# Retention decay and norm scale moved from q and k to v's rows and the group norm's epsilon, with three edits to the feed-forward jobs

## The chip, the cores and the metric

One Trainium2 chip, one core, one launch. Of the core's engines five appear in the profile: TensorE (matmuls PE, weight loads PEld), VectorE (DVE), ScalarE (ACT), GpSimd (POOL) and SyncE (SP, which only issues transfers). The metric is the device time of a launch in microseconds; lower is better. Everything is fp32; for speed, most matmul operands are split into a high and a low fp32r part, and a product is three matmuls (high x high, high x low, low x high).

## What is computed

Two decoder layers over 544 tokens: a prompt of 512 and 8 sample sequences of 4 tokens. Layer 0 mixes by a short gated convolution, layer 1 by retention; each is followed by a gated feed-forward block. The part that the change touches is the retention layer's mixer:

```python
def retention_chunkwise(q, k, v, s0):
    log_g = jnp.log(1.0 - 2.0 ** (-5.0 - jnp.arange(H)))
    decay = jnp.where(diff >= 0, jnp.exp(jnp.maximum(diff, 0.0) * log_g), 0.0)
    ...
    scores = jnp.einsum('bhid,bhjd->bhij', qc, kc) * decay
    inner = jnp.einsum('bhij,bhjv->bhiv', scores, vc)
    cross = jnp.einsum('bhid,bhdv->bhiv', qc, S) * cross_w
    S_new = S * chunk_decay + jnp.einsum('bhjd,bhjv->bhdv', kc * state_w, vc)

def retention_mixer(x, s0, pos, w_in, gn_g, w_out):
    q, k, v, g = jnp.split(x @ w_in, ...)          # 4 heads; dk 256, dv 512
    q = rotary(q, pos)
    k = rotary(k, pos) * (HEAD_DK ** -0.5)
    o, S = retention_chunkwise(q, k, v, s0)
    mu, var = mean(o), mean((o - mu) ** 2)          # over a token's dv of a head
    of = (o - mu) * rsqrt(var + GN_EPS)             # GN_EPS = 1e-6
    return (silu(g) * (of * gn_g)) @ w_out, S
```

The input `x` is already normalized: every row of a token was multiplied by that token's rms factor. The decay between tokens i and j is a power of the head's gamma with exponent i - j, so it can be written as a factor of token i times a factor of token j.

## The kernel before

Activations are kept transposed (feature rows on the 128 partitions, 544 tokens along the free dimension, in two halves of 272). The rms factor is not applied to the input: products are made of the raw residual (times gain), and the factor R (128x2x272, one value per token, the same in each row) or rN (one column per tile of 128 tokens) is multiplied in behind the product.

**Who orders the work.** The program names what each engine does; a planner of the framework simulates it, sets the order of each engine's instructions and places the waits. Each engine then runs its own list strictly in order, and an instruction that waits holds up all behind it on that engine. A tile's tag names a ring of buffers; a new tile waits until the buffer's former readers are done. `tc.issue_after` only orders instructions of one engine.

**PSUM.** Eight banks: `psum()` takes a tile of two banks from a ring of two ("mm" in the profile), `bank()` one from a ring of four ("sm").

**The feed-forward jobs.** Gate and up products run as `Job`s: two 128-wide slices of the output at once by a scheme of seven half products in place of eight (numbers 1 to 7, 12 matmuls each, L480). `weights7` (L428) loads the two weight pieces w3 (L434) and w1 (L435), forms three differences and sums on VectorE (L438 to L440: the halves of w2, and one in place) and w4 (L441, which reads w1), and splits all four into high and low parts: `mixed` (ACT L423, DVE L424, ACT L425 and an adding DMA of POOL, L426) for w1 and w3, `split` (ACT L190, DVE L191) for w2 and w4. A job holds three sums: a (products 1, 6, 7, 4), b (product 2) and c (products 5, 3). `summed` (L533) snapshots the first three states of a (u1 to u3, ACT L540) and adds b or c to a snapshot (DVE L543). The sum c22 reads c before product 3 is added into it. In `run` (L516), a job's `prepare` (its weights) is called before the middle of the job ahead, and its first product before the end of that job.

**The stage `ahead`** (L785), at the end of layer 0's feed-forward block, makes what the retention layer will need: q and k of head 0 (four weight pieces, raw products copied to DRAM as `qk_made`), and, as five jobs, gates of heads 0, 1 and 2 (`gates`, L833; L847 multiplies with R).

**The retention heads** (loop at L1298). For head h:
- `qk_start` loads a table gt = gtab[h] (L915; 2 x 544 values in each of 128 rows, 544 KB: decay of q and of k by token), `qk_scale` multiplies its two halves by R (L942). `qk_project` projects a 128-wide piece of q or k, `qk_rotate` multiplies it out of PSUM by gt (L959), and after the second piece `rotate` makes four products with cos and sin (L969 to L972), a difference and a sum (L973, L974). For head 0, `qk_loaded` loads the raw q and k (L926), multiplies by gt (L930) and rotates, k in two halves of the tokens.
- `value` (L987) projects v into four banks, and multiplies by rN as it is split (L1037, L1038). Inside it come the scores of the sample tokens (L1198), qm (L1019) and `keys`.
- `states_update` (L1238 on TensorE, L1243 on VectorE) updates the sample states through two `psum()` tiles; `scores`, `inner` and `normalized` (group norm; the reciprocal root is an add on VectorE, L226, and a power on GpSimd, L227) make the prompt's outputs; `gated` transposes them (L1172) and multiplies by the gate.
- k and q of head h+1 are projected in between (`fill`, and after the third `inner`).

## Time and profile before

| what | value |
|---|---|
| time, median of 3 runs | 1458.92 us (1457.52 to 1459.11) |
| profiled execution: time | 1461.27 us |
| profiled execution: span of its instructions | 1459.5 us |
| mean granted TensorE clock | 0.996 |
| DMA | 201.89 MB, mean 138 GB/s |

The time of a run is a little longer than the span from the first to the last instruction. A row of a timeline has start, duration, engine, line, operation, names (out<-in), shapes, and in brackets the idle time of the engine before it with what ended that. A row by line or tile has minimum, median and maximum duration in ns after the count. A row of waits has the total, the number and the longest. A row of DMA issues has the count, the size of one and the median time from issue to landing. A matmul's recorded duration overlaps the next one's; the distance of starts tells its pace.

### The profile page before, as it was taken

What the parts mean: (1) busy time and instruction counts of PE and PEld (TensorE: products, weight loads), DVE (VectorE), ACT (ScalarE), POOL (GpSimd) and SP (SyncE); (2) the same over time, 40 slices, a digit from 0 to 9 for tenths busy, and PEclk for the clock granted to TensorE, in tenths of its full rate; (3) what the DMA queues carried; (4) which work ended last, traced back from release to release, by engine and by line L of the source; (5) the groups of instructions that cost most, each with busy time, mean ns of one, the idle gap of its engine ahead of it and who ended that gap; (6) DMA issues with size and microseconds to landing.
All of it is one profiled execution on the core that took longest, in us unless ns stands there. A gap on an engine that the chain in (4) does not pass through costs nothing.

```text
span 1459.5 us, 26302 instructions
## 1 busy us (share of the span) xinstructions
PE 1443.8 (99%) x10860; PEld 1369.0 (94%) x10860; DVE 985.7 (68%) x1536; ACT 664.0 (45%) x971; POOL 147.9 (10%) x184
## 2 busy tenths in 40 slices
PE   9999999999999999999999999999999999999997
PEld 8999999999999999997878888878999999999997
DVE  5644679847748648677575765845699848749554
ACT  5222466626526437664223032134386626537334
POOL 0100011101101003210010000000111101101002
PEclk9999999999999999999999999999999999999998
DMA  6222246636536434767353734724666635546432
GB/s 219 82 88 92 86 114 140 150 116 126 143 106 139 124 80 133 195 167 262 125 191 116 258 106 144 274 92 143 175 138 149 153 108 131 131 109 148 119 81 77
DMA packets 84297, 201.89 MB, mean 138 GB/s; under 512 B 8129, under 2 KB 25409, under 8 KB 83921
## 3 DMA queue, kind: packets, MB, share of 16 engines
q1 hardware_dynamic: 67296, 165.91, 35.9%
q0 software_dynamic: 15008, 29.18, 12.2%
q10 hardware_dynamic: 1872, 5.12, 0.9%
q8 instruction: 85, 1.39, 0.4%
q14 instruction: 36, 0.29, 0.1%
HBM read 175.11 MB, written 25.08 MB: 137 GB/s over the span
## 4 chain that ended last, share of the span: by engine, by line
PE 89%; DVE 5%; DMA 3%; ACT 1%; issue 1%; POOL 0%; SPq 0%; DVEq 0%; ACTq 0%; POOLq 0%
PE sm L480 35%; PE mm L175 33%; PE sm L175 7%; PE sm L999 2%; PE sm L1000 2%; PE sm L1001 2%; PE sm L163 2%; PE sm L164 1%; PE sm L165 1%; PE sm L1222 1%; DMA w<-in_ffgu_dram 1%; DVE wl L191 1%; DMA w<-in_rtg_dram 1%; DVE S L1243 1%; DVE ol L191 1%
## 5 line engine op out<-in xcount | busy, mean ns | idle before, releaser
L190 ACT ACTIVATE wh<-w 128x1024 fp32r<-128x1024 f32 (+4 forms) x126 | 115.8, 923 | 318.8 <-PE mm L175 204.9
L480 PE MATMUL sm<-oh,wh 128*128 128x272 f32 x744 | 215.5, 290 | 0.1
L480 PE MATMUL sm<-ol,wh 128*128 128x272 f32 x744 | 214.3, 288 | 0.7 <-DVE ol L191 0.7
L480 PE MATMUL sm<-oh,wl 128*128 128x272 f32 x744 | 213.9, 287 | 0.0
L175 PE MATMUL mm<-xh,wh 128*128 128x272 f32 x844 | 176.3, 290 | 1.1 <-ACT wh L190 1.0
L175 PE MATMUL mm<-xh,wl 128*128 128x272 f32 x844 | 174.5, 289 | 0.4 <-DMA wl<-in_rtqk_dram 0.4
L175 PE MATMUL mm<-xl,wh 128*128 128x272 f32 x844 | 173.9, 287 | 0.0
L480 PE MATMUL sm<-oh,h 128*128 128x272 f32 x568 | 164.1, 289 | 0.5 <-DVE gate L543 0.4
L480 PE MATMUL sm<-oh,l 128*128 128x272 f32 x568 | 163.5, 288 | 0.0
L480 PE MATMUL sm<-ol,h 128*128 128x272 f32 x568 | 163.5, 288 | 0.0
L273 DVE TENSOR_TENSOR x<-x,mm 128x544 f32<-128x544 f32 x90 | 64.7, 719 | 144.7 <-PE mm L175 144.7
L191 DVE TENSOR_TENSOR wl<-w,wh 128x1024 fp32r<-128x1024 f32 (+4 forms) x126 | 134.2, 1071 | 23.7 <-ACT wh L190 22.3
L480 PEld LDWEIGHTS sm<-oh,wh 128*128 128x128 f32 x744 | 139.8, 188 | 2.1 <-ACT gate L540 0.9
L423 ACT ACTIVATE wh<-w 128x1024 fp32r<-128x1024 f32 x97 | 102.8, 1060 | 83.2 <-PE sm L480 56.1
L480 PEld LDWEIGHTS sm<-ol,wh 128*128 128x128 f32 x744 | 139.8, 188 | 0.9 <-DVE ol L191 0.9
L480 PEld LDWEIGHTS sm<-oh,wl 128*128 128x128 f32 x744 | 140.3, 189 | 0.0
L426 POOL DMA_DIRECT2D wl<-in_ffgu_dram x87 | 75.6, 869 | 635.2 <-ACT wl L425 261.5
L175 PEld LDWEIGHTS mm<-xh,wh 128*128 128x128 f32 x844 | 132.2, 188 | 5.4 <-ACT wh L190 1.4
L175 PEld LDWEIGHTS mm<-xh,wl 128*128 128x128 f32 x844 | 131.6, 188 | 0.9 <-DMA wl<-in_rtqk_dram 0.6
L175 PEld LDWEIGHTS mm<-xl,wh 128*128 128x128 f32 x844 | 132.1, 188 | 0.1
L191 DVE TENSOR_TENSOR l<-w,h 128x1024 fp32r<-128x1024 f32 x98 | 93.4, 955 | 27.0 <-ACT h L190 26.4
L480 PEld LDWEIGHTS sm<-oh,h 128*128 128x128 f32 x568 | 107.2, 189 | 1.0 <-ACT wh L423 0.6
(296 smaller groups left out, 3211.8 us busy)
## 6 DMA issues: line engine op xcount, KB each, us to landing
w<-in_ffgu_dram SPq DMA_DIRECT2D x88, 512.0 KB, 3.9
wl<-in_ffgu_dram POOLq DMA_DIRECT2D x87, 256.0 KB, 4.8
w<-in_ffdn_dram SPq DMA_DIRECT2D x96, 192.0 KB, 2.5
S<-in_rets_dram SPq DMA_DIRECT2D x16, 1024.0 KB, 7.0
out_rets_dram<-S SPq DMA_DIRECT2D x16, 1024.0 KB, 4.8
w<-in_cvin_dram SPq DMA_DIRECT2D x21, 512.0 KB, 3.4
w<-in_rtqk_dram SPq DMA_DIRECT2D x16, 512.0 KB, 3.6
w<-in_rtg_dram SPq DMA_DIRECT2D x16, 512.0 KB, 4.1
```

Source lines behind the costliest of these rows:

```text
L163: nc.tensor.matmul(out, lh, rh, start=start, stop=False, skip_group_check=True)
L164: nc.tensor.matmul(out, lh, rl, start=False, stop=False, skip_group_check=True)
L175: last_product[0] = nc.tensor.matmul(half(pt, hf)[:, :HT], w[:, c], act[k][:, hf * HT : (hf + 1) * HT], start=(first and k == ks[0] and i ...
L190: h = nc.scalar.activation(dh, src, AF.Copy)
L191: last_low[0] = nc.vector.tensor_sub(dl, src, dh.bitcast(F32))
L273: last_residual[0] = nc.vector.tensor_add(xk, xk, p)
L423: nc.scalar.activation(wh, w, AF.Copy)
L426: nc.gpsimd.dma_start(wl[:, n:], src[:, n:], accum_op=ALU.add)
L480: last = nc.tensor.matmul(out, w[:, c], b, start=(first and k == 0 and i == 0), stop=(k == KP - 1 and i == 2), skip_group_check=True,)
L999: nc.tensor.matmul(out, xh[kt][:, ts_], wh[:, cw], start=(kt == 0), stop=False)
L1000: nc.tensor.matmul(out, xh[kt][:, ts_], wl[:, cw], start=False, stop=False)
L1001: last = nc.tensor.matmul(out, xl[kt][:, ts_], wh[:, cw], start=False, stop=(kt == KT - 1))
```

## The change

The rms factor and the decay are no longer multiplied into q and k. Rotated q and k stay raw. A row (token) of v is multiplied by its own rms factor, by k's decay and 1/16, and by the rms factor that k's row lacked (`fv`, one column for each of the four token tiles and the sample). A token's output then lacks its q factor; since the group norm divides it out again, only its epsilon is scaled, by the reciprocal of that factor squared (`fe`). For the sample tokens, whose states come from outside, q's factor `gs` is kept and multiplied into qm and the sample scores.

```diff
-    nc.vector.memset(expo, -0.5)
+    nc.vector.memset(expo[:, :6], -0.5)
+    nc.vector.memset(expo[:, 6:], -1.0)
...
-    def rsqrt(out, var, n):
-        nc.vector.tensor_scalar_add(out, var, EPS)
+    def rsqrt(out, var, n, eps=None):
+        if eps is None:
+            nc.vector.tensor_scalar_add(out, var, EPS)
+        else:
+            nc.vector.tensor_add(out, var, eps)
...
     def weights7(src1, src2, sw, adding=False):
-        w3, w1 = [wts.tile([P, 2 * n], F32, tag="w", name=nm("w")) for _ in range(2)]
+        w1, w3 = [wts.tile([P, 2 * n], F32, tag="w", name=nm("w")) for _ in range(2)]
...
-        w4 = sw.tile([P, n], F32, tag="w4", name=nm("w4"))
-        last_load[0] = nc.sync.dma_start(w3, src2)
-        last_load[0] = nc.sync.dma_start(w1, src1)
+        w4 = fourth[0].tile([P, n], F32, tag="w4", name=nm("w4"))
+        second_load[0] = nc.sync.dma_start(w1, src1)
+        last_load[0] = nc.sync.dma_start(w3, src2)
...
                 elif which == 5:
-                    self.c = bank()[:, :HT]
+                    self.c = self.third()[:, :HT]
...
+            fourth[0] = c1.enter_context(tc.tile_pool(name=f"ffw{layer}", bufs=2, reuse_waits="tile"))
...
+        ft = tp.tile([P, 3, P], F32, tag="gu", name=nm("ft"))
+        for t in range(4):
+            nc.sync.dma_start(ft[t * NH : (t + 1) * NH, 0, :], a["gtab"][:, 0, 1, t * P : (t + 1) * P])
+        for t in range(4):
+            nc.sync.dma_start(ft[:NH, 1, t * NS : (t + 1) * NS], a["gtab"][:, 0, 1, SEQ:])
+
+        def factors():
+            pt = bank()
+            nc.tensor.transpose(pt[:, : 4 * NH], ft[: 4 * NH, 0, :], ident[: 4 * NH, : 4 * NH])
+            nc.tensor.transpose(pt[:, 4 * NH : 5 * NH], ft[:NH, 1, :], ident[:NH, :NH])
+            tab = pt[:, : 4 * NH].rearrange("p (t h) -> p t h", h=NH)
+            ri = ft[:, 2, :4]
+            nc.gpsimd.tensor_tensor(ri, rN[:, :4], expo[:, 6:7].to_broadcast([P, 4]), op=ALU.pow)
+            scale, back = [r.unsqueeze(2).to_broadcast([P, 4, NH]) for r in (rN[:, :4], ri)]
+            nc.vector.tensor_mul(fv[:, :4, :], tab, scale)
+            nc.vector.tensor_scalar(
+                fv[:, 4, :], pt[:, 4 * NH : 5 * NH], rN[:, 5:6], rN[:, 5:6], op0=ALU.mult, op1=ALU.mult
+            )
+            nc.vector.tensor_mul(fe, tab, back)
+            nc.vector.scalar_tensor_tensor(fe, fe, 256.0 * EPS, fe, op0=ALU.mult, op1=ALU.mult)
+            nc.vector.tensor_mul(fv[:, :4, :], fv[:, :4, :], scale)
...
-            return Job([a["rtg"][h, n + i] for i in range(2)], operand, sw, summed(tile2, gate))
+            return Job([a["rtg"][h, n + i] for i in range(2)], operand, sw, summed(tile2, gate), lambda: psum()[:, 0, :])
...
-        run(jobs, (2, 5, 6), lambda i: None, iter(()))
+        run(jobs, (2, 5, 6), lambda i: factors() if i == 1 else None, iter(()))
...
-        def qk_start(h):
+        def qk_places(h):
...
-            with tc.issue_after(last_load[0].ins) if h == 0 else ExitStack():
-                nc.sync.dma_start(gt, a["gtab"][h])
...
         def qk_loaded(st):
             for t, src in ((st["rot"][1], qk_made[1]), (st["rot"][0], qk_made[0])):
-                with tc.issue_after(last_load[0].ins):
+                with tc.issue_after((second_load if src is qk_made[1] else last_load)[0].ins):
                     nc.sync.dma_start(t, src)
             for which in (1, 0):
-                qk_scale(st, which)
                 r = st["rot"][which]
-                nc.vector.tensor_mul(r, r, st["gt"][:, which, :].unsqueeze(1).to_broadcast([P, 2, T]))
...
-        def qk_scale(st, which):
-            gi = halves(st["gt"][:, which, :])
-            nc.vector.tensor_mul(gi, gi, R)
...
-            each(
-                lambda p, ri, gi: nc.vector.tensor_mul(ri, p, gi), pt, halves(r[:, dt, :]), halves(st["gt"][:, which, :])
-            )
+            if dt == 0:
+                st["rt"] = products()
+            for d, by in ((st["rt"][1 - dt], sin), (r[:, dt, :], cos)):
+                each(lambda p, d, f: nc.vector.tensor_mul(d, p, f), pt, halves(d), halves(by))
             if dt:
-                rotate(r, *products())
+                turned(r, *st["rt"])
...
+        def turned(r, t0, t1):
             nc.vector.tensor_sub(r[:, 0, :], r[:, 0, :], t0)
             nc.vector.tensor_add(r[:, 1, :], r[:, 1, :], t1)
...
+                    gs = st["gs"] = one.tile([P, NS], F32, tag="gs", name=nm("gs"), bufs=1)
+                    nc.vector.tensor_mul(
+                        by_sequence(gs), by_sequence(R[:, 1, HT - NS :]), fq[:, h, :].unsqueeze(1).to_broadcast([P, NB, DS])
+                    )
...
-                nc.scalar.activation(vh[:, tt, :], pv[tt], AF.Copy, scale=rN[:, tt : tt + 1])
+                nc.scalar.activation(vh[:, tt, :], pv[tt], AF.Copy, scale=fv[:, tt, h : h + 1])
...
+            nc.vector.tensor_mul(ss, ss, st["gs"][:NS])
...
+        fq = one.tile([P, NH, DS], F32, tag="fq", name="fq")
+        nc.sync.dma_start(fq, a["gtab"][:, :, 0, SEQ : SEQ + DS].rearrange("h p s -> p h s"))
...
-            yn0 = normalized(inner(h, st, 0))
+            yn0 = normalized(inner(h, st, 0), fe[:, 0, h : h + 1])
```

The sample's v (`v4`), the low half of v, the other three prompt norms and qm follow the same pattern; two small tiles that shared a buffer (tag "vs") move with it to another pool, which keeps the pools' sizes in line with those of the stage before. Four loads of gt, every L942 and both L930 are gone, the job's third sum takes a tile of the wide ring in the gate jobs of `ahead` alone, and the order of the two weight loads and the second place for w4 hold for all jobs, those of both feed-forward blocks too.

More of the change, by code (lines that the diff above doesn't have):

```diff
@@ L127, in hybrid_decode_kernel @@
     rN = resid.tile([P, 6], F32, tag="rN", name="rN")
-    last_load = [None]
+    fv = resid.tile([P, 5, NH], F32, tag="fv", name="fv")
+    fe = resid.tile([P, 4, NH], F32, tag="fe", name="fe")
+    last_load, second_load = [None], [None]
     def parts2(n, pool=None, tags=("wh", "wl")):
@@ L461, in hybrid_decode_kernel, with __init__ @@
     class Job:
-        def __init__(self, srcs, operand, sw, take):
-            self.srcs, self.operand, self.sw, self.take = srcs, operand, sw, take
+        def __init__(self, srcs, operand, sw, take, third=None):
+            self.srcs, self.operand, self.sw, self.take, self.third = srcs, operand, sw, take, third or bank
         order = (6, 5, 2)
@@ L1058, in keys @@
                 nc.tensor.transpose(pt[:NS, 0, token_tiles(dt)], krot[:, dt, SEQ:], ident)
-            k2 = qp.tile([NS, 2, 2 * P], F32R, tag="vs", name=nm("k2"), bufs=1)
+            k2 = one.tile([NS, 2, 2 * P], F32R, tag="vs", name=nm("k2"), bufs=1)
             split(k2[:, 0, :], k2[:, 1, :], pt[:NS, 0, : 2 * P])
@@ L1091, in sample_operands @@
             placed(pt[:, 1, : 2 * P], k2[:, 0, :], k2[:, 1, :], 1)
-            vs = qp.tile([P, DV], F32R, tag="vs", name=nm("vs"), bufs=1)
+            vs = one.tile([P, DV], F32R, tag="vs", name=nm("vs"), bufs=1)
             nc.scalar.activation(vs, pt[:, 0, :], AF.Copy)
@@ L1326, in hybrid_decode_kernel @@
                 nc.sync.dma_start(st["gate"][0][:, :2, :], gate_made[0][:, :2, :])
-                nxt = qk_start(1)
-                for which in (1, 0):
-                    qk_scale(nxt, which)
+                nxt = qk_places(1)
             fill(2)
@@ L1339, in hybrid_decode_kernel @@
                 held_parts(h, older)
-            yn0 = normalized(inner(h, st, 0))
+            yn0 = normalized(inner(h, st, 0), fe[:, 0, h : h + 1])
             sample_outputs(h, st, 1)
-            yn1 = normalized(inner(h, st, 1))
+            yn1 = normalized(inner(h, st, 1), fe[:, 1, h : h + 1])
             states_update(h, st, 1)
@@ L1346, in hybrid_decode_kernel @@
             if more and h:
-                nxt = qk_start(h + 1)
-                for which in (1, 0):
-                    qk_scale(nxt, which)
+                nxt = qk_places(h + 1)
             with tc.issue_after(last_product[0].ins):
```

35 lines of the change are left out of this document (17 added, 18 removed).

## The prediction

> **What bounds the kernel now.** I read the page first: the engines' shares and the chain that ended last.
>
> ```profile
> span 1459.5 us, 26302 instructions
> PE 1443.8 (99%) x10860; PEld 1369.0 (94%) x10860; DVE 985.7 (68%) x1536; ACT 664.0 (45%) x971; POOL 147.9 (10%) x184
> PE 89%; DVE 5%; DMA 3%; ACT 1%; issue 1%; POOL 0%; SPq 0%; DVEq 0%; ACTq 0%; POOLq 0%
> ```
>
> TensorE carries 89% of the chain and idles 1459.5 - 1443.8 = 15.7 us. An edit that takes work from VectorE or a DMA queue is worth only what TensorE waited for it, so I looked for TensorE's idle time in the stages that the change touches: the work for the next layer at the end of the first feed-forward block (about 560 to 656 us), then the four retention heads. The view by stretches has busy time of PE, PEld, DVE, ACT, POOL, then clock, DMA share and GB/s.
>
> ```profile
> 560.00:656.00 96.00, 93.46 (x718) 91.51 (x718) 73.57 (x123) 66.70 (x101) 20.38 (x20) 0.98 0.66 179
> 656.00:1050.00 394.00, 393.74 (x2543) 324.69 (x2541) 255.41 (x395) 114.44 (x151) 17.50 (x22) 1.00 0.51 171
> ```
>
> The heads leave 394.00 - 393.74 = 0.26 us idle: where most of the edited lines run there is almost nothing to win, only something to lose. The stage ahead leaves 2.54 us, at a clock of 0.98. TensorE's timeline has three waits there:
>
> ```profile
> 592.28 0.52 PE L175 MATMUL mm<-xh,wl 128*128 128x272 f32 x2 [0.36 <-DMA wl<-in_rtqk_dram]
> ...
> 626.75 0.29 PE L480 MATMUL sm<-xh,wl 128*128 128x272 f32 x1
> 627.41 0.36 PE L480 MATMUL sm<-oh,h 128*128 128x272 f32 x1 [0.37 <-DVE gate L543]
> ...
> 632.67 0.29 PE L480 MATMUL sm<-ol,wh 128*128 128x272 f32 x1
> 632.80 0.29 PE L480 MATMUL sm<-oh,wl 128*128 128x272 f32 x1
> 634.88 0.39 PE L480 MATMUL sm<-xh,h 128*128 128x272 f32 x1 [1.80 <-DVE gate L543]
> ```
>
> Starts normally stand 0.13 us apart, so the third wait costs 634.88 - 632.80 - 0.13 = 1.95 us and the second 627.41 - 626.75 - 0.13 = 0.53 us. The third has a tail: from about 636.0 the clock reads 0.50 for 3.4 us and starts stand 0.225 us apart.
>
> ```profile
> 636.00:639.40 3.40, 3.40 (x18) 3.40 (x17) 3.15 (x6) 1.35 (x2) 0.02 (x1) 0.50 0.69 105
> ...
> 637.08 0.43 PE L480 MATMUL sm<-oh,l 128*128 128x272 f32 x1
> 637.30 0.43 PE L480 MATMUL sm<-oh,h 128*128 128x272 f32 x1
> ```
>
> In 3.4 us go 3.4 / 0.225 = 15 matmuls, each 0.10 us late: 1.5 us more. So 1.95 + 1.5 + 0.53 = 4.0 us hang on two waits.
>
> Why the third happened stands in VectorE's timeline just before, and in SP's:
>
> ```profile
> 625.09 0.69 DVE L441 TENSOR_TENSOR w<-w,w 128x512 f32<-128x512 f32 x1
> 625.70 1.22 DVE L191 TENSOR_TENSOR l<-w,h 128x1024 fp32r<-128x1024 f32 x1
> ...
> 627.78 0.69 DVE L438 TENSOR_TENSOR w<-w 128x512 f32<-128x512 f32 x1
> 629.65 0.69 DVE L439 TENSOR_TENSOR w<-w,w 128x512 f32<-128x512 f32 x1 [1.18 <-DMA w<-in_rtg_dram]
> 630.26 0.69 DVE L440 TENSOR_TENSOR w<-w,w 128x512 f32<-128x512 f32 x1
> 631.24 1.36 DVE L942 TENSOR_TENSOR gt<-gt,R 128x544 f32<-128x544 f32 x2 [0.29 <-DMA gt<-in_gtab_dram]
> 633.19 1.29 DVE L930 TENSOR_TENSOR rot<-rot,gt 128x1088 f32<-128x1088 f32 x1 [0.59 <-DMA rot<-qkm]
> 634.40 0.43 DVE L543 TENSOR_TENSOR gate<-gate,sm 128x272 f32<-128x272 f32 x1
> ```
> ```profile
> 625.85 0.33 SPq L435 DMA_DIRECT2D w<-in_rtg_dram  x1
> 626.23 0.43 SPq L915 DMA_DIRECT2D gt<-in_gtab_dram  x1
> 626.70 0.42 SPq L926 DMA_DIRECT2D rot<-qkm  x1
> ```
>
> The sum c22 (L543, at 634.40) must read its bank before TensorE adds product 3 into it. VectorE works in order, and ahead of it stood head 0's key scaling: a wait for the table, two L942, a wait for the keys, one L930. SP's rows also say why all was late: w1's load (L435, 625.85) goes out right after L441 ends (625.09 + 0.69), since L441 is the last reader of the w1 before, and L441 itself stood behind the split of the one w4.
>
> **The change, part by part.**
>
> *Tables gone.* Four gt loads, eight L942 and two L930 vanish; a projection is multiplied by sin and cos straight from PSUM.
>
> ```profile
> L942 DVE TENSOR_TENSOR gt<-gt,R x8: 705/716/725, 631.2 to 920.5; 128x544 f32<-128x544 f32 x8
> L930 DVE TENSOR_TENSOR rot<-rot,gt x2: 1291/1292/1294, 633.2 to 659.2; 128x1088 f32<-128x1088 f32 x2
> ```
>
> VectorE loses 8 x 0.72 + 2 x 1.29 = 8.3 us, and 12 projections lose one multiplication of 128x544 each, 0.72 us as L942's, 8.7 us; together 17 us. In the heads this is worth nothing (0.26 us idle). Ahead of c22 it is worth a wait: the removed instructions alone are 1.36 + 1.29 = 2.65 us, more than the 1.95 us by which c22 came late, and the keys no longer share the queue with a 544 KB table. **-1.95 us**, and the slow tail with it: the gap of 0.37 us at 627.41 is followed by no drop of the clock (1.00 from 627 to 628), the one of 1.80 us is. **-1.5 us.**
>
> [...]
>
> *Two places for w4, w1 loaded before w3.* L441 need not wait for the split of the w4 before; it can run right after L440. In the 625 us stretch that takes 0.69 us out from in front of the L191 at 625.70, for which product 5 or 6 at 627.41 waited: **-0.53 us**, at worst 0. The first sum, L438, now reads the second load. Both orders made VectorE wait for a late load:
>
> ```profile
> DVE w L439 <- DMA w<-in_ffgu_dram: 10.9, 17, 2.4
> DVE w L439 <- DMA w<-in_rtg_dram: 2.1, 3, 1.2
> ```
>
> These waits would move one instruction (0.69 us) earlier in the order, but the load leaves as soon as w1 is free, some us earlier. In the feed-forward blocks TensorE did not pay for them before, so **0**; at that block's start it paid once, after residuals queued behind such a wait:
>
> ```profile
> 204.84 0.39 PE L480 MATMUL sm<-ol,wh 128*128 128x272 f32 x1 [0.66 <-DVE ol L191]
> ```
>
> That could go or double: -0.8 to +0.8, taken as 0.
>
> *Third sums in the wide banks.* Only makes room for the bank that `factors` takes: 0.
>
> *`factors`.* Two transposes on TensorE, at most 0.27 us each by the row below, less when streamed: **+0.2**. Its eight small table loads stand on SP before the first gate weights; one issue is 0.33 us, 8 x 0.33 = 2.7 us, and SP has the stretch from 566.79 + 0.33 to 569.79 free, 2.67 us. Those weights feed products from about 598, so 0. Its VectorE work is six instructions, each smaller than L543's 0.43 us; one waits for POOL's reciprocal, whose nearest row is L227 (0.54 us median, 3.0 at worst). c22 has about 24 matmuls x 0.13 = 3 us of cover (the next job's product 1 and this one's product 4), so the bounds are 0 and 6 x 0.43 + 3.0 - 3 = +2.6; with the median wait the cover is not used up, and I take 0.
>
> ```profile
> L1172 PE MATMUL mm<-cb,yn x64: 270/272/329, 732.6 to 1042.1; 128*128 128x128 f32 x64
> L227 POOL TENSOR_TENSOR rs<-rs,expo x20: 537/544/3008, 717.8 to 1037.6; 128x1 f32<-128x1 f32 x20
> 566.79 0.33 SPq L145 DMA_DIRECT2D w<-in_rtqk_dram  x1
> 569.79 0.33 SPq L434 DMA_DIRECT2D w<-in_rtg_dram  x1
> ```
>
> *PSUM read twice.* This is where the change can lose. A projection's bank used to be free after one L959, now after two. In head 0 the state updates L1238 sit directly behind it:
>
> ```profile
> 712.24 0.19 PEld L1238 LDWEIGHTS mm<-vs,kns 32*128 32x128 f32 x4 [0.86 <-DVE rot L959]
> 722.14 0.19 PEld L1238 LDWEIGHTS mm<-vs,kns 32*128 32x128 f32 x4 [0.37 <-DVE rot L959]
> ...
> 711.15 0.72 DVE L959 TENSOR_TENSOR rot<-mm,gt 128x544 f32<-128x544 f32 x1 [3.78 <-PE mm L175]
> 721.32 0.72 DVE L959 TENSOR_TENSOR rot<-mm,gt 128x544 f32<-128x544 f32 x1 [2.14 <-PE mm L175]
> ```
>
> The second read ends about 0.64 us later (instructions of this size follow each other at that distance: 2 x 0.72 overlap to 1.36 in the L942 row): 712.5 and 722.7 instead of 711.87 and 722.04. TensorE was at L1238 at 712.24 and 722.14, so it waits 0.4 + 0.64 = 1.0 us if the instruction order stays, 0 if the planner puts matmuls of the inner product in front. I take **+0.3**, nearer to 0, as those matmuls are ready there. The other projections' banks are next asked for several us later.
>
> *The rest.* Scales of v read another column; the epsilon becomes a column, one small instruction for another; gs, the extra multiplication of the sample scores and fq's load (16-byte pieces, but wanted 20 us later) lie beside the value projection: 0, and were the 32x32 multiplication waited for in each head, less than 4 x 0.43 = +1.7 by L543's row. The second memset at the start lies before the first input has landed: 0.
>
> **Sum:** -1.95 - 1.5 - 0.53 + 0.2 + 0.3 = -3.5 us. Against the profiled execution (span 1459.5, 1461.27 with what lies around it) that is 1457.8; its time is 2.35 above the median of the runs shown, 1458.92, and I assume that those lose the same 4.0 us: 1458.92 - 3.5 = **1455.4 us**. With one cost at its dear end, `factors`, it is 1458.0, with the two dearest (2.6 + 1.7) 1459.7; with all at 0 and the waits at 592.28 and 204.84 gone too (0.36 + 0.66), 1453.9.
>
> **The rivals.**
>
> [...]
>
> *The rotation still holds c22 up.* Keys are rotated by VectorE right after their load lands, 5.4 us after issue in the median; if the planner again puts them before c22, part of the 1.95 stays, and with over 1 us of idle the slow tail too. Then only 0.5 to 1 us is won, and the PSUM cost eats half: about 1458.4. Against: the 2.65 us of instructions are gone for certain.
>
> *Slower: the last w3 behind the keys.* The key load is now tied to the first weight load of the last job, so it may leave SP before the second. Its 544 KB take 5.4 us to land (4.1 for a weight), and L438, first in line, waits for w3.
>
> ```profile
> rot<-qkm SPq DMA_DIRECT2D x2, 544.0 KB, 5.4
> w<-in_rtg_dram SPq DMA_DIRECT2D x16, 512.0 KB, 4.1
> ```
>
> If w3 lands when the keys would have (up to 6.4 - 4.1 = 2.3 us later) and c22 of the job before stands behind L438, today's 1.95 us grows to 4.3 and draws a second slow stretch: 2.3 + 1.5 + 0.5 (transposes, PSUM) on top: 1463.2. It decides once w3 comes more than the 3 us of cover after L438's turn. For it: L439 already waited 1.18 us in just this place. Against: w1 is freed earlier, so both loads leave some us sooner.
>
> **How the numbers follow.** The forecast 0.60, the half clock that stays 0.06, the rotation that still holds 0.14, slower 0.20. What this kernel's measurement can tell from no change is about 0.2%, 2.9 us: faster means below 1456.0, slower above 1461.8. Of the forecast's own range, 1453.9 to 1458.0, I put nine tenths below 1456.0, because each dear end needs a cover to fail: faster 0.54. The rest of it (0.06) and the two middle rivals (0.20): same 0.26; slower 0.20. The range 1453.6 to 1460.0 holds the first three cases and the two dearest costs.
>
> **What would show it.** In the changed trace: no wait on L543 near 635 and a clock of 1.00 all through 560 to 656; PE busy within 1 us of that stretch; no DMA of gt; L441's successor running right after L440; the second load leaving before the job's last difference does today. L1238's waits in head 0 give the price of the second PSUM read. The forecast is wrong if a gap of over 1 us with half clock stands elsewhere, or if the heads' stretch is longer by more than 1 us.

## The result: slower, and the profile after

The changed kernel takes 1471.24 us (median of 4 runs, 1469.61 to 1474.04); the kernel before took 1458.88 beside it. The ratio is 1.0089, 95% interval 1.0071 to 1.0106: 12.4 us are lost. The page of the changed kernel (time of this execution 1469.61 us, the fastest of the four):

```profile
span 1467.8 us, 26317 instructions
PE 1448.5 (99%) x10862; PEld 1371.0 (93%) x10862; DVE 971.7 (66%) x1531; ACT 664.8 (45%) x971; POOL 144.8 (10%) x185
PE 88%; DVE 4%; DMA 3%; issue 3%; ACT 1%; POOL 1%; DVEq 0%; SPq 0%; POOLq 0%; ACTq 0%
```

The work that was to vanish did vanish: VectorE is busy 14.0 us less than before (985.7; the prediction put the removed work at 17), and DMA moves 199.68 MB in place of 201.89. Yet TensorE idles 1467.8 - 1448.5 = 19.3 us, 3.6 more, and is busy 4.7 us longer with two more matmuls. The two stretches of the prediction, in the view by stretches:

```profile
560.00:656.00 96.00, 93.12 (x727) 91.02 (x726) 72.17 (x118) 65.85 (x99) 23.11 (x20) 1.00 0.67 176
656.00:1050.00 394.00, 392.89 (x2515) 321.97 (x2514) 244.45 (x394) 114.42 (x153) 14.21 (x23) 1.00 0.48 165
```

The stage ahead has no half clock any more (1.00 in place of 0.98), but 2.88 us idle where there were 2.54; the heads idle 1.11 in place of 0.26. TensorE's timeline shows where (the bracket has the idle time in front and what ended it):

```profile
211.28 0.39 PE L492 MATMUL sm<-oh,wh 128*128 128x272 f32 x1 [1.31 <-ACT g L552]
490.08 0.39 PE L492 MATMUL sm<-oh,wh 128*128 128x272 f32 x1 [1.12 <-ACT u L552]
596.41 0.52 PE L181 MATMUL mm<-xh,wl 128*128 128x272 f32 x2 [1.09 <-DMA wl<-in_rtqk_dram]
638.17 0.39 PE L492 MATMUL mm<-xh,h 128*128 128x272 f32 x1 [0.66 <-DVE gate L555]
644.65 0.39 PE L492 MATMUL mm<-oh,l 128*128 128x272 f32 x1 [0.65 <-DVE l L197]
1091.69 0.39 PE L492 MATMUL sm<-oh,wl 128*128 128x272 f32 x1 [1.32 <-DVE wl L433]
```

The wait of 1.80 us at 634.88 is gone, and these six, each of more than 0.6 us, are new or longer than before. Three of them stand in the feed-forward blocks (211, 490 and 1091), where no line of the retention layer runs.

A ledger shows what idle rows leave out. TensorE's matmuls were numbered in order of start (the change adds two of about 10,860), and the time between the same two numbers was compared. The profile of before that the prediction used has a stretch of half clock; the reference here is therefore the kernel before with 256 unused bytes (an experiment below), which was timed once, at 1458.26 us, and has none. Each column is one profiled execution. Further columns are experiments told below; "repaired" is the last of them, and its profiled execution (1457.34 us) was the fastest of its 11 runs.

| stretch of TensorE's work | before, us | changed | heads alone | jobs alone | order back | order alone | repaired |
|---|---|---|---|---|---|---|---|
| start, matmuls 0 to 250 | 34.79 | +0.35 | 0.00 | -0.01 | -0.24 | -0.56 | -0.08 |
| convolution, 250 to 1100 | 105.78 | +0.95 | +0.95 | 0.00 | +0.47 | 0.00 | +0.47 |
| block 0 begins, 1560 to 1700 | 18.21 | +1.03 | -0.29 | +4.18 | +4.16 | -0.25 | -0.28 |
| its gates end, 3600 to 3900 | 37.68 | +1.37 | -0.01 | +1.03 | -0.01 | 0.00 | -0.01 |
| q and k of head 0, 4600 to 4700 | 13.10 | +1.24 | -0.03 | +0.45 | +0.08 | +1.08 | -0.34 |
| gates' jobs, 4700 to 4950 | 32.37 | -0.27 | +0.50 | -0.60 | -0.48 | -0.02 | -0.47 |
| last two jobs, 4950 to 5100 | 21.21 | -0.18 | -1.38 | -1.39 | -0.84 | +0.08 | -0.91 |
| v of head 0, 5100 to 5400 | 52.01 | +0.72 | +1.38 | +1.04 | -0.11 | +0.32 | -0.21 |
| rest of head 0, 5400 to 5700 | 41.53 | +2.15 | +2.14 | -0.01 | +2.13 | -0.01 | +0.06 |
| heads 1 to 3, 5700 to 7700 | 308.56 | +0.51 | +0.67 | +0.76 | +0.29 | +0.05 | -0.10 |
| block 1 begins, 7700 to 8100 | 50.26 | +2.30 | +0.10 | +2.53 | +0.14 | +3.84 | +0.14 |
| everything else | 729.06 | +1.00 | +0.13 | -0.05 | -0.15 | +2.53 | +0.63 |
| sum | 1444.55 | +11.17 | +4.16 | +7.94 | +5.43 | +7.06 | -1.10 |

The 4.18 and 4.16 at block 0's start hold a stretch of half clock, as does the 3.84 of order alone.

### The profile page after: what moved, and what is told of

The parts are those of the page before. It is cut to its first block, busy times and chain, and to the rows that moved or that the text cites. A ratio compares the mean times of both kernels' runs of the same rounds, so it can differ in the third digit from the quotient of the medians.

```text
span 1467.8 us, 26317 instructions
## 1 busy us (share of the span) xinstructions
PE 1448.5 (99%) x10862; PEld 1371.0 (93%) x10862; DVE 971.7 (66%) x1531; ACT 664.8 (45%) x971; POOL 144.8 (10%) x185
## 2 busy tenths in 40 slices
DMA packets 84312, 199.68 MB, mean 136 GB/s; under 512 B 8640, under 2 KB 25936, under 8 KB 83936
## 3 DMA queue, kind: packets, MB, share of 16 engines
q8 instruction: 85, 1.39, 0.4%
## 4 chain that ended last, share of the span: by engine, by line
PE 88%; DVE 4%; DMA 3%; issue 3%; ACT 1%; POOL 1%; DVEq 0%; SPq 0%; POOLq 0%; ACTq 0%
PE mm L181 34%; PE sm L492 33%; PE sm L181 6%; PE sm L1027 2%; PE sm L1026 2%; PE sm L1028 2%; PE sm L169 2%; PE sm L171 1%; PE sm L170 1%; PE sm L1255 1%; PE mm L492 1%; DVE S L1276 1%; DMA wl<-in_rtqk_dram 1%; DVE wl L197 0%; PE mm L1034 0%
## 5 line engine op out<-in xcount | busy, mean ns | idle before, releaser
L181 PE MATMUL mm<-xh,wh 128*128 128x272 f32 x844 | 175.9, 290 | 0.0
L181 PE MATMUL mm<-xh,wl 128*128 128x272 f32 x844 | 174.8, 288 | 1.1 <-DMA wl<-in_rtqk_dram 1.1
L181 PE MATMUL mm<-xl,wh 128*128 128x272 f32 x844 | 174.9, 288 | 0.3 <-DVE xl L211 0.3
L492 PE MATMUL sm<-ol,h 128*128 128x272 f32 x548 | 157.8, 288 | 0.1
L492 PE MATMUL sm<-oh,h 128*128 128x272 f32 x548 | 157.8, 288 | 0.0
L492 PE MATMUL sm<-oh,l 128*128 128x272 f32 x548 | 157.7, 288 | 0.0
L197 DVE TENSOR_TENSOR wl<-w,wh 128x1024 fp32r<-128x1024 f32 (+4 forms) x126 | 134.6, 1072 | 25.2 <-ACT wh L196 23.3
L181 PEld LDWEIGHTS mm<-xh,wh 128*128 128x128 f32 x844 | 133.0, 189 | 3.7 <-DVE S L1276 0.9
L181 PEld LDWEIGHTS mm<-xh,wl 128*128 128x128 f32 x844 | 132.4, 188 | 1.7 <-DMA wl<-in_rtqk_dram 1.3
L181 PEld LDWEIGHTS mm<-xl,wh 128*128 128x128 f32 x844 | 132.4, 188 | 0.5 <-DVE xl L211 0.5
L197 DVE TENSOR_TENSOR l<-w,h 128x1024 fp32r<-128x1024 f32 x98 | 93.5, 954 | 26.3 <-ACT h L196 25.9
L492 PEld LDWEIGHTS sm<-ol,h 128*128 128x128 f32 x548 | 103.2, 188 | 0.5 <-DVE ol L197 0.5
```

Of the source, the lines that this page charges most:

```text
L181: last_product[0] = nc.tensor.matmul(half(pt, hf)[:, :HT], w[:, c], act[k][:, hf * HT : (hf + 1) * HT], start=(first and k == ks[0] and i ...
L197: last_low[0] = nc.vector.tensor_sub(dl, src, dh.bitcast(F32))
L492: last = nc.tensor.matmul(out, w[:, c], b, start=(first and k == 0 and i == 0), stop=(k == KP - 1 and i == 2), skip_group_check=True,)
```

## The experiments

In each, "before" is the kernel before, run beside it on the same chip; all times are medians.

### Which half of the change: heads alone, jobs alone

Heads alone is the changed kernel with the three job edits undone:

```diff
-        w1, w3 = [wts.tile([P, 2 * n], F32, tag="w", name=nm("w")) for _ in range(2)]
+        w3, w1 = [wts.tile([P, 2 * n], F32, tag="w", name=nm("w")) for _ in range(2)]
...
-        w4 = fourth[0].tile([P, n], F32, tag="w4", name=nm("w4"))
+        w4 = sw.tile([P, n], F32, tag="w4", name=nm("w4"))
...
-            return Job([a["rtg"][h, n + i] for i in range(2)], operand, sw, summed(tile2, gate), lambda: psum()[:, 0, :])
+            return Job([a["rtg"][h, n + i] for i in range(2)], operand, sw, summed(tile2, gate))
```

> The changed kernel with its job edits undone (w3 loaded first, one place for w4, the third sum in the common bank); the retention edits stay. Theory J (the job edits made the loss, by re-ordering ScalarE and VectorE where the blocks begin): of the +12.4 us, the part by matmul index that lies in the retention remains, +2.1 in head 0 and about +1 where factors stands, so 1460 to 1463, and the TensorE gaps of 1.1 to 1.3 us near 490 and 1091 are gone. Theory R (the retention edits made it): 1467 to 1472, with those gaps or others of their size still there.

Measured 1462.99 against 1458.2, ratio 1.0036 (1.0023 to 1.0049): 4.8 us lost. Jobs alone is the kernel before with those three edits, and nothing else:

> The kernel before with the job edits alone (w1 loaded first, two places for w4, the third sum of the gates' jobs in banks of its own). Theory J: 1464 to 1470, the gaps near 211, 490 and 1091 as in the changed kernel. Theory R: 1454 to 1458, since the stall near 627 and perhaps the one near 635 go and nothing new comes. If both parts are guilty and add up, this run and the heads-alone run together lose about 12 us.

Measured 1465.64, ratio 1.0047 (1.0032 to 1.0061): 7.4 us, with six runs spread from 1460.83 to 1468.39. 4.8 + 7.4 = 12.2 of the 12.4: both halves cost time, the jobs more, and in total they add up, though not stretch by stretch. The 1.3 us gap at the start of block 0 stands in jobs alone too (at 209.86), with 6.8 us of half clock behind it; the one at block 1's start also (1088.87). The gaps at 211, 490 and 1091 are all missing from heads alone. Of the three job edits, the wide bank for the third sum was not run by itself; the last kernel below keeps it and is level with the kernel before.

### The load order, and the second place for w4

Two kernels undo one job edit each in the changed kernel: order back (w3 first again) and w4 back (one place, in `sw`).

> The changed kernel with the load order alone put back (w3 before w1). Theory O (the order of the two loads is what shifted the conversions, so that a block begins with a gap): 1462 to 1466, gaps at 211, 490 and 1091 back to at most 0.4 us. Rival W (the second place for w4 lets the load conversions run further ahead and sit before the snapshots on ScalarE): 1469 to 1472, gaps unchanged.

> The changed kernel with w4 alone put back to one place. Theory O: 1469 to 1472, gaps at 211, 490 and 1091 unchanged, and a stall of about 0.5 us near 627 again. Rival W: 1462 to 1466, those gaps gone.

Order back: 1463.9, ratio 1.0036 (1.0024 to 1.0048). W4 back: 1467.34, ratio 1.0068 (1.0056 to 1.0080). Neither theory fits alone: the gap at 1091 goes with the order (it stays with w4 back, 1088.70, 1.31 us), the one at 211 goes with w4 (with order back it is at 209.80), and the one at 490 is in neither kernel. Beside heads alone (ratio 1.0036), the second place without the swap adds nothing that the times can tell (1.0036), the swap without the second place some 0.3% (1.0068), and both some 0.5% (1.0089), so they are not separate. The order alone, put into the kernel before; the two tiles are taken from their ring in the other order too:

```diff
-        w3, w1 = [wts.tile([P, 2 * n], F32, tag="w", name=nm("w")) for _ in range(2)]
+        w1, w3 = [wts.tile([P, 2 * n], F32, tag="w", name=nm("w")) for _ in range(2)]
...
+        nc.sync.dma_start(w1, src1)
         last_load[0] = nc.sync.dma_start(w3, src2)
-        last_load[0] = nc.sync.dma_start(w1, src1)
```

> The kernel before with one edit: w1 is loaded before w3. Theory O1 (the order alone makes the gap of 1.3 us at the second feed-forward block's start, and waits of about 1 us near 590): 1460.5 to 1463, gap near 1085 there. Rival: the order costs only together with the other edits: 1457.5 to 1459.

1463.29, ratio 1.0040 (1.0028 to 1.0053): 5.2 us for the swap, with the gap at 1084.49 (1.32 us) and 1.0 us of wait near 592. Two more waits stand in block 1, at 1234.91 and 1257.32 (0.47 and 1.12 us); the changed kernel has neither, and they make most of the 2.53 us of "everything else".

The gap at block 1's start ends with VectorE's half (L433) of a weight split. What it splits is w1 of the block's second job: the load that reuses the buffer leaves right behind it. The rows of both engines and that load, first in the changed kernel, then the same work in the kernel before:

```profile
1083.25 1.06 ACT L432 ACTIVATE wh<-w 128x1024 fp32r<-128x1024 f32 x1
1085.89 0.68 DVE L450 TENSOR_TENSOR w<-w,w 128x512 f32<-128x512 f32 x1
1087.20 0.69 DVE L451 TENSOR_TENSOR w<-w,w 128x512 f32<-128x512 f32 x1
1088.15 1.64 DVE L197 TENSOR_TENSOR ol<-f,oh 128x816 fp32r<-128x816 f32 x2
1090.34 0.69 DVE L452 TENSOR_TENSOR w<-w,w 128x512 f32<-128x512 f32 x1
1090.94 0.69 DVE L433 TENSOR_TENSOR wl<-w,wh 128x512 fp32r<-128x512 f32 x1
1091.71 0.33 SPq L446 DMA_DIRECT2D w<-in_ffgu_dram  x1
```
```profile
1077.52 1.05 ACT L423 ACTIVATE wh<-w 128x1024 fp32r<-128x1024 f32 x1
1079.57 0.68 DVE L424 TENSOR_TENSOR wl<-w,wh 128x512 fp32r<-128x512 f32 x1
1080.87 0.68 DVE L439 TENSOR_TENSOR w<-w,w 128x512 f32<-128x512 f32 x1
1084.02 0.68 DVE L440 TENSOR_TENSOR w<-w,w 128x512 f32<-128x512 f32 x1
1084.62 0.68 DVE L441 TENSOR_TENSOR w<-w,w 128x512 f32<-128x512 f32 x1
```

Before, VectorE's half (L424) starts 1.0 us after ScalarE's half (L423) has ended, ahead of the differences L439 to L441. In the changed kernel it starts 6.6 us after, behind these differences (now L450 to L452) and the last conversions of the activations (L197), and TensorE waits for it. The kernel with the order alone shows the same, with the two halves at 1076.05 and 1083.76. So the planner built another order around the swap; why it chose this one is not shown.

### Why a second place for w4 costs time at the start of block 0

VectorE's rows for the difference w4 at block 0's start, in the changed kernel:

```profile
203.02 0.69 DVE L452 TENSOR_TENSOR w<-w,w 128x512 f32<-128x512 f32 x1 [0.77 <-PE mm L181]
210.55 0.68 DVE L452 TENSOR_TENSOR w<-w,w 128x512 f32<-128x512 f32 x1
```

In the kernel before, the first two ran at 187.39 and 199.59. Now the first waits until 203.02 for the last matmuls of the convolution layer's output (L181): the instruction reads nothing that TensorE writes, so it waits for the place, which these still read. How the late difference leads to the gap at 211.28, which ends with a snapshot on ScalarE, I did not follow row by row. Three experiments took this further. W4 gates: a second place in the new pool for the gates' jobs alone, the feed-forward blocks keep one there.

> The kernel with the load order put back, and the second place for w4 used by the gates' jobs alone; the feed-forward blocks keep one. Theory W0 (the second place lets the planner split the first job's weights ahead of the residuals, and that is the gap of 1.3 us at 210, with a half clock behind it in some runs): gap at 210 at most 0.2 us, 1461 to 1462.7. Rival: the gap comes from the pool that w4 lies in, not from the number of places: 1463 to 1464.2, gap still there.

1463.74, ratio 1.0037 (1.0024 to 1.0050), gap unchanged (210.22, 1.31 us): it is not the number of places. Then two places inside `sw`:

```diff
+        w4 = sw.tile([P, n], F32, tag="w4", name=nm("w4"), bufs=2)
```

> The kernel with the load order put back, and both places of w4 in the pool sw, where the one place was before. Theory S (the gap at 210 comes from where the new pool lies: the first difference w4 waits until 202 for matmuls that still read what lies there): the first job's difference runs near 187 as before, the gap at 210 is at most 0.2 us, no half clock behind it, 1460.5 to 1462.3. Rival: two places do it, wherever they lie: 1463 to 1464.5, gap at 210 still 1.3 us.

1473.54, ratio 1.0105 (1.0091 to 1.0119): both theories missed by 10 us. The differences are early again (186.65), but 2 KB more in `sw` move the pools behind it, the operands' among them, and the operands are made late. ScalarE's first conversions of them, here and before:

```profile
198.54 2.74 ACT L196 ACTIVATE oh<-f 128x544 fp32r<-128x544 f32 x4
```
```profile
163.23 0.66 ACT L190 ACTIVATE oh<-f 128x544 fp32r<-128x544 f32 x1 [0.45 <-DVE f L409]
```

They come 35 us later, and seven gaps and two stretches of half clock follow between 203 and 227. The one other kernel with both places in `sw` (below) shows the same, and none of the rest does. Last, w4 of the feed-forward blocks in `sw` as before, and only every other w4 of the gates in the new pool:

```diff
+        w4 = (fourth[0] if second and turn[0] % 2 else sw).tile([P, n], F32, tag="w4", name=nm("w4"))
```

> The kernel with the load order put back, where w4 of the feed-forward jobs lies in sw as before and only every other w4 of the gates' jobs lies in the new pool, which has one place. Theory S2 (a w4 in the new pool waits at the first block for the last matmuls of the stage before, since it lies on their weights): the first two differences run near 187 and 199 again, no gap over 0.2 us at 210, no half clock behind it: 1460.5 to 1462.5. Rival: the pool's being there moves other tiles, and the block's start stays late: 1463 to 1465 or worse.

1461.57, ratio 1.0019 (1.0010 to 1.0028), 2.3 us less than order back; the differences run at 187.23 and 199.09, and no gap over 0.13 us stands near 210. W4 gates and this kernel both have one place for the blocks' w4; they differ in where it lies, so that is what costs.

### The second read of PSUM

Heads alone, with each projection copied out of PSUM once:

```diff
-            for d, by in ((st["rt"][1 - dt], sin), (r[:, dt, :], cos)):
-                each(lambda p, d, f: nc.vector.tensor_mul(d, p, f), pt, halves(d), halves(by))
+            each(lambda p, d: nc.vector.tensor_copy(d, p), pt, halves(r[:, dt, :]))
             if dt:
-                turned(r, *st["rt"])
+                rotate(r, *products())
```

> The heads-alone kernel with each projection read from PSUM once: VectorE copies the bank into r, and the second half of a pair is rotated from SBUF as before. Theory P (the second PSUM read cost head 0 its 2.1 us): head 0's stretch shrinks by 2.0 us or a little more, so 1460.5 to 1461.5. Rival Q (head 0 lost its time to something else, such as the loads now missing or the keys coming later): 1462.5 to 1464, head 0 unchanged.

1460.29, ratio 1.0014 (1.0005 to 1.0023), 2.7 us less than heads alone; the rest of head 0 goes from +2.14 to +0.13. TensorE's rows in the changed kernel, and below them the same work with one read:

```profile
725.48 0.50 PE L1271 MATMUL mm<-vs,kns 32*128 32x512 f32 x2
725.91 1.02 PE L1255 MATMUL sm<-S,qm 128*8 128x512 f32 x2
726.87 0.50 PE L1271 MATMUL mm<-vs,kns 32*128 32x512 f32 x2
727.29 1.04 PE L1255 MATMUL sm<-S,qm 128*8 128x512 f32 x6
728.26 0.50 PE L169 MATMUL sm<-mid,qkhl 128*128 128x512 f32 x1
```
```profile
721.57 0.51 PE L1267 MATMUL mm<-vs,kns 32*128 32x512 f32 x4
722.01 1.04 PE L1251 MATMUL sm<-S,qm 128*8 128x512 f32 x8
722.98 0.50 PE L169 MATMUL sm<-mid,qkhl 128*128 128x512 f32 x1
```

The same 12 matmuls take 728.26 - 725.48 = 2.78 us and 722.98 - 721.57 = 1.41 us. No row shows more idle time. In the kernel before, the four of 32 rows at 722.14 start at 722.139, .143, .146 and .149, and the next matmul at 722.569: a group of four in 0.43 us. The eight with 8 columns behind them start in two such groups of four, 6 to 7 ns apart, which take 0.43 and 0.54 us. By their starts, these three groups became six groups of 2, 1, 1, 2, 3 and 3 in the changed kernel, and they take 0.43, 0.43, 0.52, 0.43, 0.43 and 0.54 us. In the rest of head 0, 48 such matmuls stand in 12 groups before (5.63 us) and in 16 groups in the changed kernel (7.41 us): 1.8 of the 2.15 us. That the planner broke the groups because it saw a bank come free later is my reading; the runs show only that they are whole again with one read.

### The place and bank of `factors`

Heads alone has a gap of 0.97 us at 618.63 that ends with the write of fe. With `factors()` called after the last job and not after the second:

> The heads-alone kernel with factors() called after the last of the five jobs instead of after the second. Theory F (the gap of 0.97 us at 618.6, put down to the write of fe, is factors holding a bank): that gap goes, 1461.5 to 1462.3. Rival: the wait is moved to where the heads begin, 1462.5 to 1464, with a new gap of about 1 us near 655.

1462.9, ratio 1.0036 (1.0023 to 1.0048): nothing won. The gap went, and a longer one came in the last jobs, behind a ScalarE instruction of a gate:

```profile
642.03 0.36 PE L492 MATMUL sm<-oh,h 128*128 128x272 f32 x1 [1.38 <-ACT gate L884]
```

### 144 bytes

The first stretch that heads alone loses, the convolution layer, has no changed line in it. What did change is that fv and fe (80 + 64 bytes per partition) lie behind rN. The kernel before with that much, unused, and one with 256 bytes:

```diff
     rN = resid.tile([P, 6], F32, tag="rN", name="rN")
+    pad = resid.tile([P, 36], F32, tag="pad", name="pad")
+    nc.gpsimd.memset(pad, 0.0)
```

> The kernel before with 144 bytes per partition added behind rN, as fv and fe add them, and one memset. Theory L (the 0.95 us that the first 750 matmuls behind the start lost comes from tiles lying 144 bytes further on): these matmuls take 1.0 us longer than before, 94.2 us where they took 93.3. Rival: unchanged, 93.3, and the loss comes from something else at the start.

> The kernel before with 256 bytes per partition added behind rN in place of 144. Theory A (what costs is where tiles start against a multiple of 64 bytes or more): the 750 matmuls behind the start take 93.3 us again. Rival: any shift costs: 94.2 us as with 144 bytes.

The 750 matmuls (250 to 1000) took 93.33 us before, 94.17 with 144 bytes, 93.33 with 256 (one execution each). The view by stretches from 40 to 120 us, for before, 144 and 256 bytes; the count behind PE is what was done in 80 us:

```profile
40.00:120.00 80.00, 80.00 (x645) 80.00 (x644) 42.52 (x69) 21.41 (x24) 7.90 (x20) 1.00 0.27 86
```
```profile
40.00:120.00 80.00, 80.00 (x640) 80.00 (x639) 41.80 (x68) 21.26 (x24) 7.13 (x20) 1.00 0.25 86
```
```profile
40.00:120.00 80.00, 80.00 (x645) 80.00 (x645) 42.53 (x68) 20.70 (x24) 7.99 (x20) 1.00 0.25 86
```

TensorE is busy all the time in each, at a clock of 1.00; with 144 bytes it does 640 matmuls in place of 645. The kernels with 144 and 256 bytes differ in the size of the unused tile alone. But 256 bytes were no remedy in the next runs: with fv and fe filled to that size, the same matmuls took 94.58 us (637 in the 80 us, in heads alone with four repairs, below), and in the kernel with w4 twice in `sw`, 144 bytes on, 93.33. Others lie between: the alternate kernel takes 0.41 us more than before, and order back does 643 in the 80 us. What sets the pace is not shown.

### Are the losses separate? All repairs together

> The changed kernel with two repairs, one read of PSUM and 256 bytes; all job edits stay. If these losses are 2.1 and 1.0 us in the changed kernel too: 1467 to 1469.5, head 0's stretch and the 750 matmuls behind the start as before the change. Rival: among the other waits they are hidden: 1470 to 1473.

The changed kernel with one PSUM read and 256 bytes: 1469.59, ratio 1.0072 (1.0059 to 1.0084). The rest of head 0 falls from +2.15 to +0.17; the fill made the convolution worse (+1.42).

> All repairs together: load order and third sums as before, both places of w4 in sw, one read of PSUM for each projection, factors' bank from the wide banks, and fv and fe filled up to 256 bytes. If the losses found so far are separate and add up: the heads-alone kernel's 1463.0 less 2.1 (PSUM), less 0.9 (bank of factors), less 1.0 (bytes), less about 1 (keys early again): 1457 to 1458.5, below or level with the kernel before. If repairs only move the waits on, as the late factors did: 1459.5 to 1461.

1473.39, ratio 1.0098 (1.0083 to 1.0114): far outside both ranges: it has both places of w4 in `sw`, and with them the late operands told above.

> The same with one read of PSUM for each projection and fv and fe filled up to 256 bytes. If the three losses are separate: 2.1 and 1.0 us less than the alternate kernel, so 1457.5 to 1459.5. If a repair moves the wait on: 1460 to 1462.

The alternate kernel with one PSUM read and the fill: 1459.42, ratio 1.0002 (0.9993 to 1.0011).

> The heads-alone kernel with one read of PSUM (1460.3 so far), fv and fe filled up to 256 bytes, factors' bank from the wide banks, and an unused tile of 4352 bytes where the table gt stood, so that the keys' place is free early again. If all four losses are separate: 1460.3 less 1.0 (bytes), 0.9 (bank), 1.0 (keys): 1457 to 1458.5, level with the kernel before or a little below it. If repairs move waits on: 1458.5 to 1460.5.

Heads alone with four repairs: 1461.47, ratio 1.0020 (1.0012 to 1.0029), more than with the PSUM repair alone and outside both expected ranges: a wait of 1.34 us stands at 639.82, and the keys still come late (at 652.69). The last two kernels, without the fill, tell the keys apart. Neither is heads alone; both build on the alternate kernel:

> The alternate kernel with one read of PSUM for each projection, and fv and fe without fill. Theory: only the PSUM term goes, 2.0 us less than the alternate kernel's 1461.6, so 1459 to 1460; and since the fill to 256 bytes made the 750 matmuls behind the start slower here (1.25 us over before, 0.41 without), it is not above the filled version's 1459.4 by more than noise: 1458.3 to 1459.6. Rival: 1460.5 or more.

> The same, with an unused tile of 4352 bytes where gt stood and the tiles vs back in the pool they came from, so that the heads' pools start where they did before. Theory K (the gap of 1.2 to 1.4 us near 665, where the sample scores wait for the rotated keys, comes from the keys' place, which lies on tiles that TensorE reads until 650): the keys are loaded near 625 again and that gap goes: 1457 to 1458.5, level with the kernel before or up to 1 us below it. Rival: the load still leaves near 650 and the time is that of the version without the unused tile.

1459.44, ratio 1.0006 (0.9997 to 1.0015), and 1459.0, ratio 1.0003 (0.9994 to 1.0012). SP's row of the keys' load and TensorE's of the sample scores in the first, and SP's in the second:

```profile
651.12 0.33 SPq L958 DMA_DIRECT2D rot<-qkm  x1
...
665.70 0.25 PE L1226 MATMUL mm<-rot,rot 128*32 128x32 f32 x2 [1.14 <-DVE rot L997]
```
```profile
622.51 0.42 SPq L961 DMA_DIRECT2D rot<-qkm  x1
```

With the heads' pools where they were, the keys load 29 us earlier and the gap at 665 is gone: the change had moved the keys' own tile, by gt's removal and the move of the tag vs together, and its load had to wait (the unused tile alone, in the kernel with four repairs, did not help). The time hardly shows it: 0.4 us less, which is smaller than either kernel's spread, and it stays above the 1457 to 1458.5 expected. This last kernel no longer has the changed load order, the second w4 of the feed-forward blocks and the double read of PSUM, and it keeps the memory that gt took. Its profiled execution is 1.1 us shorter than the reference of the ledger, but it is its fastest; over 11 runs it is level with the kernel before. No version beat that kernel.

## Why the prediction was wrong, point by point

**The step that failed** is the one on the jobs: "In the feed-forward blocks TensorE did not pay for them before, so 0; at that block's start ... -0.8 to +0.8, taken as 0", together with "-0.53 us, at worst 0" for the second place of w4. Jobs alone lost 7.4 us. I priced the waits of the one instruction that moves (0.69 us). I did not price that the planner makes a new order around it (VectorE's half of a split 6.6 us behind ScalarE's at block 1's start, where it was 1.0), nor that a tile in a new pool lies on other tiles of the stage before. The order alone costs 5.2 us. The small wait behind the -0.53 us did go in the changed kernel, but it is gone from heads alone as well, without a second place.

**Tables gone, the stall at 634.88:** right in its mechanism. The wait is gone, and heads alone shows it without the job edits: the last two jobs take 1.38 us less than in the reference, in which the wait is 1.45 us. Jobs alone, with the tables, gains 1.39 there too, so either half removes it. With both, other waits took most of it back (0.66 and 0.65 us at 638 and 645; the stretch gains 0.18).

**The half clock behind it, -1.5 us:** counted where it was not. The sum assumed that the runs shown lose it too. Of 11 runs of before beside the first four experiments, ten have a mean clock of 0.997 or 0.998, and one 0.995, at 1462.78; the profile of the prediction had 0.996. The reference has the stall (1.45 us) and full clock behind it. So the half clock was a property of that execution (0.98 over 560 to 656 us, 1.00 in the reference), and the median has nothing to win there. I had set the sum against a profile 2.35 us above the median and taken off a gain that explains most of this difference.

**PSUM read twice, +0.3, bounds 0 to 1.0:** mis-sized, and outside its bounds: 2.1 us. TensorE does not wait at the state updates (L1238, now L1271), as in my case "0 if the planner puts matmuls of the inner product in front"; but the new order breaks groups of small matmuls, and that is dearer than the 1.0 us at which I had bounded the wait.

**`factors`, 0, bounds to +2.6:** within its bounds (which counted six instructions on VectorE; there are five). Its bank costs 0.97 us at 618 in heads alone; in the changed kernel, where it has a free bank, TensorE waits 1.09 us at 596 in place of 0.36 at 592. But the order alone has 1.00 us there as well, so little of this is left for the eight loads, which leave SP from 586.28 on and not near 567; no run has them alone. Placed later, `factors` saves nothing.

**What no step held:** the 0.95 us of the convolution layer, most of which the kernel before shows with 144 unused bytes (94.17 us in place of 93.33); and in heads alone 1.21 us at 666.44 for keys that load late, since their tile had moved. The prediction's own sign of being wrong did come: from v of head 0 to the end of head 3 the changed kernel takes 0.72 + 2.15 + 0.51 = 3.4 us longer.

**The rivals.** Two of them happened in small. In the changed kernel the keys leave SP at 622.41 and w3 at 627.40. VectorE's rows:

```profile
633.14 0.69 DVE L449 TENSOR_TENSOR w<-w 128x512 f32<-128x512 f32 x1 [1.76 <-DMA w<-in_rtg_dram]
...
636.98 0.44 DVE L993 TENSOR_TENSOR rot<-rot,sqacc 128x272 f32<-128x272 f32 x1
637.33 0.44 DVE L997 TENSOR_TENSOR rot<-rot,rt 128x272 f32<-128x272 f32 x1
637.69 0.43 DVE L555 TENSOR_TENSOR gate<-gate,mm 128x272 f32<-128x272 f32 x1
```

VectorE waits for w3 behind the keys ("the last w3 behind the keys", the slower one), and a part of the rotation stands ahead of the sum c22 (L555; "the rotation still holds c22 up"). Yet TensorE waits 0.66 us for c22, not the 4.3 of the slower case. The whole time fell outside all cases, 8 us above the dearest. The half clock did not stay, to which the prediction gave 0.06: with the gap at 634.88 gone, the changed kernel reads 1.00 from 560 to 656. A gap can stand without it: those of 1.09 us at 596.41 and 1.12 at 490.08 have a clock of 1.00 behind them, so the "over 1 us of idle" that was to bring the slow tail back was an estimate that these do not bear out. With order back it does stand behind a gap of 1.30 us, at 209.80; the view by stretches behind it reads:

```profile
210.80:217.60 6.80, 6.80 (x32) 6.80 (x32) 4.75 (x9) 1.36 (x3) 2.45 (x2) 0.50 0.72 194
217.60:224.40 6.80, 6.80 (x58) 6.80 (x57) 3.02 (x4) 3.97 (x7) 0.91 (x1) 1.00 0.42 108
```

58 - 32 = 26 matmuls at 0.13 us, 3.4 us, were lost in it.

## What to carry to other kernels

In a kernel whose bound engine is 99% busy, an edit to shared helpers is paid in every place that calls them: price the order that the planner may make, not the instruction that moves, and test each half of a change by itself. A new tile, a removed one, or a few bytes move everything allocated behind them; ask what lies under each tile, and what reads it last. Set a forecast against the median's own state, not against a stall that one profiled execution happens to show.

## What the runs showed of the hardware

**Half clock stands behind some gaps of 1.3 us and not behind others.** In the profile of before, the clock reads half for 3.41 us from 636.03 on, behind a gap of 1.80 us (at 634.88). With order back it reads 0.50 from 210.80 to 217.60, behind 1.30 us (at 209.80); with jobs alone from 211.00 to 217.80, behind 1.31 (at 209.86); with order alone from 1084.90 to 1088.30, behind 1.32 (at 1084.49). In the changed kernel gaps of the same size, 1.31 us at 211.28 and 1.32 at 1091.69, have 1.00 behind them, and the reference, with its wait of 1.45 us, reads 1.00 from 560 to 656. So idle time alone does not decide it; what else does is not shown. Two traces show when it starts. Before, the clock first reads full at 4.57 us and goes to half 631.47 us later (at 636.03, for 3.413 us), then full again for 812.37 us, up to 1.6 us behind TensorE's last matmul; in the changed kernel it first reads full at 6.18 and stays so for 1454.08 us, up to 1.7 us behind the last matmul. The three full stretches are 185, 238 and 426 times 3.413 us long, to within 0.04 of one; no more than that is shown. Equal runs differ: jobs alone had 1460.83 at a mean clock of 0.998 and 1468.39 at 0.993.

**A lower pace without a wait.** The 750 matmuls of an unchanged stage took 94.17 us in place of 93.33 in the kernel with 144 unused bytes, at a clock of 1.00 and with no idle row. Busy shares do not show it (80.00 of 80 us in both); the count of matmuls in a stretch does (640 and 645), and so do starts compared number by number. In the rest of head 0, a group of small matmuls (32 rows or 8 columns, 512 elements) took 0.43 to 0.54 us with four in it, and 0.40 to 0.54 with one to three: broken groups cost time in which TensorE counts as busy (42.00 of 42 us from 703 to 745 in both kernels).
